# A fourth group of the down projection by seven products, with three chunks' token sums taken from DRAM

## The chip, the cores and the metric

The kernel runs on one core of a Trainium2 chip. Its engines work side by side, each through its own instruction list in order: TensorE multiplies (PE; its weight loads are shown as PEld), VectorE (DVE) and ScalarE (ACT) do elementwise work, GpSimd (POOL) and SyncE (SP) mostly issue transfers. The metric is the device time of one execution, in microseconds; lower is better. Three runs of the kernel before gave a median of 1541.31 us.

## The reference

One decoder layer for 256 tokens of width 2048: a mixer, then a gated MLP, then a final norm. The change touches the end of the MLP and the norm:

```python
h = rmsnorm(x, norm_ffn_w[l])
gate, up = jnp.split(jnp.einsum('bsd,df->bsf', h, w_up[l]), 2, axis=-1)
gate = causal_dwconv(gate, conv_ffn_w[l]) + conv_ffn_b[l]
x = x + jnp.einsum('bsf,fd->bsd', jax.nn.gelu(gate, approximate=False) * up, w_down[l])
return rmsnorm(x, norm_final_w)
```

The down projection `w_down` has 5632 rows and 2048 columns, in float32.

## The kernel before

**Float32 by two halves.** TensorE multiplies in a shorter format, so each weight block is split into a high part (`whi`, a cast on ScalarE, line 289) and a low part (`wlo`, the block less its high part, on VectorE, line 297). The activations are split too. A product of two float32 blocks is then three matmuls: high by high, high by low, low by high (`products`, line 1356). A weight block is 256 rows by 512 columns, 512 KB, and a matmul has 512 columns. `whi` and `wlo` have three buffers each: the cast for a block waits until TensorE has left the block three before it, and so TensorE is never more than two blocks behind the splits.

**The down projection.** The 5632 rows are eleven chunks of 512, and the 2048 columns two halves of 1024 (`half`, or `hf`). One chunk in one half is four blocks (two of rows, two of columns), and the tokens are two sets of 128. Most chunks are *plain*: each of the four blocks meets both token sets, 12 matmuls a block, 48 in all. The chunks in `SEVEN` take *seven products* instead of eight (Strassen's scheme in Winograd's form): three of the products use a block as it is (`11`, `22`, `21`), four use sums of blocks (`T1` to `T4`), and some use sums over the two token sets on the other side. A product is 6 matmuls, so such a chunk takes 42. For that VectorE makes four block sums in place (`quad`, line 283), and all seven operands are split, where a plain chunk has four splits. Once per chunk the token sums are made (`half_sums`, line 1292, with `four_sums`, line 1274): four sums, a cast, a low part; both halves use them. Before the change the chunk's activations are first put together again from their two parts (line 1299) for chunks 8 and 9, and chunk 10 keeps its float32 tile.

**The order of the work.** `stream` writes the order by hand: `gaps` is the number of plain blocks ahead of each group of seven products, and inside a group one plain block follows each product except the first. In the second half, four blocks of the last plain chunks are loaded and split early and kept (`keep`; `khi`, `klo`) for the end of the kernel. Within this order a scheduler at build time may let one engine's instruction go ahead of another's, as matmuls of neighbouring blocks do.

**Transfers.** Plain and kept blocks come by SP's queue into four buffers (`raw`, line 209). The blocks of the seven products (`quad`, line 243) are issued by POOL, whose list also holds the reload of the residual (`xt`, `xtl`, line 1555). There are eight homes for them; a group's block 11 and 12 take the homes of 22 and 21 of two groups back, and its 22 and 21 those of 12 and 11 of the group before. POOL waits at each issue until the home is free, and all that stands behind waits too.

**The end of a half.** When the last group of a half is through, a chain of four adds (`u`, lines 1575 to 1580) and four additions to the residual (`plus`, line 1504) joins the partial results. In the first half the finished columns are then multiplied by the final norm's weights (`weighted`, line 1511).

## Time and profile before

| | |
|---|---|
| median of three runs | 1541.31 us (1539.55 to 1541.64) |
| the profiled execution, whole | 1542.63 us |
| its span, first to last instruction | 1540.8 us |
| TensorE busy | 1526.0 us, 99% of the span |
| VectorE busy | 1253.4 us, 81% |
| ScalarE busy | 849.8 us, 55% |
| down projection, from its first matmul | 1299.0 us after the span's start |
| granted TensorE clock | 0.999 |

A row of the timeline gives the start and duration in microseconds, the engine, the line of the program, the operation, output and inputs, and in brackets the idle time before it with what ended it. A row of the chain of waits gives start, duration and the instruction that carried the end at that moment, with the number of instructions. A row of the windows gives the stretch, its length, and each engine's busy time in it with its instructions.

### The profile page before, as it was taken

How to read it: one execution, taken by the hardware profiler on the slowest of the kernel's cores; microseconds unless marked ns; L12 is line 12 of the kernel's file. 1: busy time of each engine (PE TensorE's matmuls, PEld its weight loads, DVE VectorE, ACT ScalarE, POOL GpSimd, SP SyncE). 2: the span in 40 equal slices, each digit the busy share in tenths (PEclk: the TensorE clock that was granted, in tenths of full speed). 3: DMA queues.
4: the chain of work that ended last, by engine and by line, in shares of the span. 5: the costliest groups of instructions: out<-in, count | busy, mean ns of one | idle time of the engine just before them, and what ended most of it. 6: DMA issues, size and time to landing. Idle time of an engine off the chain costs nothing.

```text
span 1540.8 us, 20209 instructions
## 1 busy us (share of the span) xinstructions
PE 1526.0 (99%) x7302; PEld 1257.4 (82%) x7302; DVE 1253.4 (81%) x1776; ACT 849.8 (55%) x1063; POOL 70.8 (5%) x90
## 2 busy tenths in 40 slices
PE   9999999999999999999999999999999999999998
PEld 8887888788878888788888888888788888888886
DVE  6788859896589858987667899999999886878885
ACT  7455446454455445454455676666667665555552
POOL 1010002000100000000000000000000000000100
PEclk9999999999999999999999999999999999999999
DMA  8776757776577766776578646666457467556652
GB/s 276 215 221 199 202 163 214 213 214 183 152 245 205 205 169 201 222 200 186 179 250 300 194 163 217 219 205 205 150 155 242 125 216 267 183 193 205 227 189 90
DMA packets 166674, 310.46 MB, mean 201 GB/s; under 512 B 19458, under 2 KB 23330, under 8 KB 166446
## 3 DMA queue, kind: packets, MB, share of 16 engines
q1 hardware_dynamic: 159456, 287.37, 60.0%
q0 software_dynamic: 5184, 18.88, 3.7%
q10 hardware_dynamic: 1934, 2.93, 0.5%
q8 instruction: 57, 0.93, 0.2%
q14 instruction: 43, 0.35, 0.1%
HBM read 301.75 MB, written 7.38 MB: 201 GB/s over the span
## 4 chain that ended last, share of the span: by engine, by line
PE 92%; DVE 4%; issue 2%; DMA 1%; ACT 0%; POOL 0%; POOLq 0%; DVEq 0%; ACTq 0%
PE psg L1374 25%; PE psm L334 15%; PE psm L332 14%; PE psm L333 14%; PE psm L1359 7%; PE psg L1359 7%; DVE wlo L297 3%; PE psm L1374 2%; PE psm L478 1%; PE psg L377 1%; DVE quad L230 1%; PE psm L1436 1%; DMA vrow<-ev 1%; PE psg L868 1%; DMA mv<-vrow 1%
## 5 line engine op out<-in xcount | busy, mean ns | idle before, releaser
L289 ACT CAST whi<-raw 128x1024 fp32r<-128x1024 f32 x428 | 450.0, 1052 | 428.4 <-PE psm L333 280.2
L297 DVE TENSOR_TENSOR wlo<-raw,whi 128x1024 fp32r<-128x1024 f32 x426 | 517.3, 1220 | 151.2 <-ACT whi L289 146.2
L289 ACT CAST whi<-quad 128x1024 fp32r<-128x1024 f32 x168 | 176.1, 1054 | 141.0 <-DVE quad L230 39.4
L297 DVE TENSOR_TENSOR wlo<-quad,whi 128x1024 fp32r<-128x1024 f32 x168 | 202.6, 1219 | 36.2 <-ACT whi L289 35.3
L334 PE MATMUL psm<-wlo,xhl 128*128 128x512 f32 x432 | 169.5, 393 | 1.6 <-DVE wlo L297 1.6
L332 PE MATMUL psm<-whi,xhl 128*128 128x512 f32 x432 | 169.0, 391 | 0.0
L333 PE MATMUL psm<-whi,xhl 128*128 128x512 f32 x432 | 168.6, 390 | 0.0
L1374 PE MATMUL psg<-whi,fhl 128*128 128x512 f32 x504 | 127.1, 389 | 0.0
L1374 PEld LDWEIGHTS psg<-whi,fhl 128*128 128x128 f32 x504 | 94.4, 188 | 19.5
L334 PEld LDWEIGHTS psm<-wlo,xhl 128*128 128x128 f32 x432 | 81.1, 188 | 19.0 <-DVE wlo L297 2.4
L333 PEld LDWEIGHTS psm<-whi,xhl 128*128 128x128 f32 x432 | 81.1, 188 | 16.8
L332 PEld LDWEIGHTS psm<-whi,xhl 128*128 128x128 f32 x432 | 81.1, 188 | 16.6
L230 DVE TENSOR_TENSOR quad<-quad,quad 128x1024 f32<-128x1024 f32 x72 | 87.6, 1217 | 0.0
L1374 PE MATMUL psg<-wlo,fhl 128*128 128x512 f32 x252 | 69.9, 389 | 0.0
L1374 PE MATMUL psg<-whi,ups 128*128 128x512 f32 x216 | 58.9, 394 | 0.0
L1359 PE MATMUL psm<-whi,hhi 128*128 128x512 f32 (+1 forms) x150 | 58.1, 387 | 0.0
L1359 PE MATMUL psm<-whi,hlo 128*128 128x512 f32 (+1 forms) x150 | 57.9, 386 | 0.0
L1359 PE MATMUL psm<-wlo,hhi 128*128 128x512 f32 (+1 forms) x150 | 57.4, 387 | 0.1
L1374 PEld LDWEIGHTS psg<-wlo,fhl 128*128 128x128 f32 x252 | 47.3, 188 | 9.8
L332 PE MATMUL psm<-whi,mhi 128*128 128x512 f32 x128 | 50.8, 397 | 0.0
L1359 PE MATMUL psg<-whi,hhi 128*128 128x512 f32 (+1 forms) x130 | 50.3, 387 | 0.4 <-ACT whi L289 0.4
L1359 PE MATMUL psg<-whi,hlo 128*128 128x512 f32 (+1 forms) x130 | 50.0, 386 | 0.0
(432 smaller groups left out, 2927.3 us busy)
## 6 DMA issues: line engine op xcount, KB each, us to landing
raw<-in_w_in_dram SPq DMA_DIRECT2D x224, 512.0 KB, 4.2
raw<-in_w_up_dram SPq DMA_DIRECT2D x104, 512.0 KB, 4.8
quad<-in_w_up_dram SPq DMA_DIRECT2D x72, 512.0 KB, 4.9
raw<-in_w_down_dram SPq DMA_DIRECT2D x64, 512.0 KB, 4.7
raw<-in_w_out_dram SPq DMA_DIRECT2D x32, 512.0 KB, 4.2
quad<-in_w_down_dram POOLq DMA_DIRECT2D x24, 512.0 KB, 5.5
mv<-vrow SPq DMA_DIRECT2D x12, 512.0 KB, 4.9
taps<-in_conv_qkv_w_dram SPq DMA_DIRECT2D x16, 256.0 KB, 6.8
```

The source lines that it names most:

```text
L230: nc.vector.tensor_tensor(out_, plus_, minus_, op=ALU.subtract)
L289: nc.scalar.copy(hi, raw)
L297: last_split[0] = nc.vector.tensor_tensor(lo, raw, hi.bitcast(F32), op=ALU.subtract).ins
L332: mm(ps[:, t, :], lh(k, t), hi[:, kk, :], start=(k == 0), stop=False)
L333: mm(ps[:, t, :], ll(k, t), hi[:, kk, :], start=False, stop=False)
L334: mm(ps[:, t, :], lh(k, t), lo[:, kk, :], start=False, stop=(k == nk - 1))
L377: nc.tensor.transpose(pt[:, ff, t * P : (t + 1) * P], src[:, t, f * P : (f + 1) * P], ident)
L478: mm(ps_k0[:, t, :], part(k, t), w[:, kk, :], start=(k == 0 and w is hi and part is xh), stop=(k == KD - 1 and w is lo))
L868: mm(pg0, kq[:, h, 0, 0:P], kq[:, h, :, :], start=True, stop=True)
L1359: mm(ps[:, cs], lhs(kk), part_[:, kk, cs], start=(first and kk == 0 and n == 0), stop=(last and kk == 1 and n == 2), skip_group_check=shared)
L1374: mm(ps, lhs(kk), w[n][:, kk], start=(first and n == 0 and kk == 0 and lhs is high), stop=False, skip_group_check=True)
L1436: nc.tensor.transpose(out_[f // 2][:, f % 2, t * P : (t + 1) * P], e[:, t, f * P : (f + 1) * P], ident)
```

## The change

A fourth chunk, number 7, leaves the plain ones and goes by seven products, in both halves. The first half takes the chunks in the order 8, 9, 10, 7, the second 7, 8, 9, 10. The number of plain blocks inside a group is no longer six: `FIVE` and `FOUR` say after which products one stands, so that groups have five, four or three, and the gaps between groups are shorter. The kept blocks move to after plain block 8, 12, 16 and 20 of the second half. The four activations that a seven-product chunk needs in float32 are no longer joined from two parts: chunks 7, 8 and 9 are written to DRAM when they are made and read back (`bring`) ahead of their token sums. The tile `x0`, which held the final norm's weights, now holds chunk 7's token sums; the weights are read later, on POOL's queue instead of ACT's, and the first half's columns are multiplied by them after the last split of the kernel.

```diff
-    SEVEN = (8, 9, 10)
+    SEVEN = ((8, 9, 10, 7), (7, 8, 9, 10))
...
-        for n, chunk in zip(gaps, SEVEN):
+        for (n, behind), chunk in zip(gaps, SEVEN[half]):
             plain(n)
             for i, what in enumerate(PRODUCTS):
                 steps[half].append(("part", chunk, what))
                 srcs.append((half, chunk, what))
-                if i:
+                if i in behind:
                     plain(1)
         plain(len(todo))
...
-    stream(0, DIRECT, (6, 3, 3))
-    stream(1, DIRECT[:-2], (3, 1, 1), (9, 13, 17, 21))
+    FIVE, FOUR = (1, 2, 3, 4, 5), (1, 3, 4, 6)
+    stream(0, DIRECT, ((6, FIVE), (1, FIVE), (1, FOUR), (1, (1, 3, 4))))
+    stream(1, DIRECT[:-2], ((3, FIVE), (0, FOUR), (0, FOUR), (0, FOUR)), (8, 12, 16, 20))
...
+    y_d = {c: dpool.tile([P, 4, S], F32, tag=f"y{c}", bufs=1, name=f"y{c}") for c in (7, 8, 9)}
+
+    def bring(c):
+        if c != 10:
+            whole[c] = fp.tile([P, 4, S], F32, tag={8: "hlo10", 9: "eu", 7: "y"}[c], name=nm("whole"))
+            nc.gpsimd.dma_start(whole[c], y_d[c])
...
-            h = fp.tile([P, 4, S], F32, tag="hlo10" if c == SEVEN[0] else "eu", name=nm("whole"))
-            nc.vector.tensor_tensor(h, hhi[c].bitcast(F32), hlo[c].bitcast(F32), op=ALU.add)
+            h = whole[c]
...
             nc.vector.tensor_tensor(y[:, fs], pt, y[:, fs], op=ALU.mult)
+        if c in y_d:
+            nc.gpsimd.dma_start(y_d[c], y)
...
-    nfin = big.tile([P, D], F32, tag="x0", name="nfin")
-    nc.scalar.dma_start(nfin, norm_final_w.partition_broadcast(P))
...
+            if hf and what == "22" and chunk == SEVEN[hf][1]:
+                nfin.append(big.tile([P, D], F32, tag="x0", name="nfin"))
+                nc.gpsimd.dma_start(nfin[0], norm_final_w.partition_broadcast(P))
+            if hf == 0 and what == "11" and chunk != SEVEN[0][-1]:
+                bring(SEVEN[0][SEVEN[0].index(chunk) + 1])
...
                     plus(t, c, own[c, t])
                     squared(t, c, c)
-                    weighted(t, c)
...
+    for t in range(2):
+        for c in range(2):
+            with tc.issue_after(last_split[0]):
+                weighted(t, c)
     ws += wk
```

Over the whole program TensorE's list loses 12 matmuls of 512 columns and VectorE's gains 17 instructions, ScalarE's gains seven casts and loses one transfer, SP's loses eight transfers of 512 KB and POOL's gains fifteen: eight `quad`, three writes and three reads of the chunks kept in DRAM, and the norm's weights. Nothing ahead of the down projection is moved except that these few stand in between.

Three places show it. The names are the program's, with the number of the buffer; `quad<-quad` with two tiles is a block sum, `wlo` the low part of a block, `klo` of a kept block, `raw` a plain block.

VectorE at the end of the first half's last group, from the split of product 21 on, before:

```order
L297 TENSOR_TENSOR wlo_11965<-quad_11752,whi_11963 128x1024
L1575 TENSOR_TENSOR u_12034<-u_12034,psg_11455 128x512
L297 TENSOR_TENSOR wlo_11977<-raw_11973,whi_11975 128x1024
L283 TENSOR_TENSOR quad_11752<-quad_11752,quad_11684 128x1024
L1576 TENSOR_TENSOR u_12034<-u_12034,psg_11426 128x512
L1504 SCALAR_TENSOR_TENSOR xt_11610<-u_12034,rs_7231,xt_11610 128x512
L1578 TENSOR_TENSOR u_12034<-u_12034,psg_11363 128x512
L297 TENSOR_TENSOR wlo_11994<-quad_11752,whi_11992 128x1024
L1580 TENSOR_TENSOR u_12034<-u_12034,psg_11363 128x512
L1504 SCALAR_TENSOR_TENSOR xt_11612<-u_12034,rs_7231,xt_11612 128x512
L297 TENSOR_TENSOR wlo_12008<-raw_12004,whi_12006 128x1024
```

And the same place after:

```order
L299 TENSOR_TENSOR wlo_12025<-quad_11866,whi_12023 128x1024
L1592 TENSOR_TENSOR u_12076<-u_12076,psg_11461 128x512
L285 TENSOR_TENSOR quad_11866<-quad_11866,quad_11817 128x1024
L1593 TENSOR_TENSOR u_12076<-u_12076,psg_11432 128x512
L1516 SCALAR_TENSOR_TENSOR xt_11560<-u_12076,rs_7231,xt_11560 128x512
L1595 TENSOR_TENSOR u_12076<-u_12076,psg_11369 128x512
L299 TENSOR_TENSOR wlo_12036<-quad_11866,whi_12034 128x1024
L1597 TENSOR_TENSOR u_12076<-u_12076,psg_11369 128x512
L1516 SCALAR_TENSOR_TENSOR xt_11562<-u_12076,rs_7231,xt_11562 128x512
L299 TENSOR_TENSOR wlo_12056<-raw_12052,whi_12054 128x1024
```

The split of a plain block between product 21 and the sum for T4 is gone: no plain block stands between these two products now.

VectorE at the end of the second half's second group and the start of the next, before:

```order
L297 TENSOR_TENSOR wlo_12497<-quad_12308,whi_12495 128x1024
L297 TENSOR_TENSOR wlo_12509<-raw_12505,whi_12507 128x1024
L283 TENSOR_TENSOR quad_12308<-quad_12308,quad_12249 128x1024
L297 TENSOR_TENSOR klo_12570<-raw_12566,khi_12568 128x1024
L297 TENSOR_TENSOR wlo_12526<-quad_12308,whi_12524 128x1024
L297 TENSOR_TENSOR wlo_12540<-raw_12536,whi_12538 128x1024
L297 TENSOR_TENSOR wlo_12558<-raw_12554,whi_12556 128x1024
```

And after:

```order
L299 TENSOR_TENSOR wlo_12459<-quad_12340,whi_12457 128x1024
L285 TENSOR_TENSOR quad_12340<-quad_12340,quad_12269 128x1024
L299 TENSOR_TENSOR wlo_12470<-quad_12340,whi_12468 128x1024
L299 TENSOR_TENSOR wlo_12490<-raw_12486,whi_12488 128x1024
L299 TENSOR_TENSOR wlo_12512<-quad_12363,whi_12510 128x1024
L285 TENSOR_TENSOR quad_12363<-quad_12398,quad_12363 128x1024
L285 TENSOR_TENSOR quad_12398<-quad_12431,quad_12398 128x1024
```

The sum for T4 and the low part of that sum now stand next to each other, and one plain block, not two, lies before the next group's product 11; the kept block's low part has moved to before T2's, ahead of these rows.

POOL in the second half, before:

```order
L243 DMA quad_12308<-in_w_down_dram 128x2x512
L243 DMA quad_12249<-in_w_down_dram 128x2x512
L1555 DMA xtl<-xtd 128x2x512 x2
L243 DMA quad_12373<-in_w_down_dram 128x2x512
L243 DMA quad_12432<-in_w_down_dram 128x2x512
```

And after:

```order
L245 DMA quad_12340<-in_w_down_dram 128x2x512
L245 DMA quad_12269<-in_w_down_dram 128x2x512
L1565 DMA nfin<-in_norm_final_w_dram 128x2048
L245 DMA quad_12363<-in_w_down_dram 128x2x512
L245 DMA quad_12398<-in_w_down_dram 128x2x512
L245 DMA quad_12472<-in_w_down_dram 128x2x512
L245 DMA quad_12431<-in_w_down_dram 128x2x512
L1572 DMA xtl<-xtd 128x2x512 x2
```

The norm's weights now stand between the blocks of the second group and those of the third, whose issues follow them on POOL.

More of the change, by code (lines that the diff above doesn't have):

```diff
@@ L149 @@
     down = [cols(w_down[0], 512 * c, KF) for c in range(4)]
-    SEVEN = (8, 9, 10)
+    SEVEN = ((8, 9, 10, 7), (7, 8, 9, 10))
     PRODUCTS = ("11", "T1", "22", "T3", "T2", "21", "T4")
-    DIRECT = [c for c in range(KF // 4) if c not in SEVEN]
+    DIRECT = [c for c in range(KF // 4) if c not in SEVEN[0]]
     LAST = DIRECT[-2:]
@@ L240, in next_quarter @@
             g, i = asked.pop(0)
-            half, chunk, what, home = g // 3, SEVEN[g % 3], ORDER[i], HOMES[g][i]
+            half, chunk, what, home = g // 4, SEVEN[g // 4][g % 4], ORDER[i], homes[g][i]
             r = (fp if home[:2] == "xt" else big).tile([P, 2, 512], F32, tag=home, name=nm("quad"))
@@ L1510, in weighted @@
     def weighted(t, c):
-        nc.vector.tensor_tensor(block(t, c), block(t, c), nfin[:, c * 512 : (c + 1) * 512], op=ALU.mult)
+        nc.vector.tensor_tensor(block(t, c), block(t, c), nfin[0][:, c * 512 : (c + 1) * 512], op=ALU.mult)
     def direct(ps, kp, t, w, first, last, **more):
@@ L1566 @@
             alone = what in ("11", "T1", "T2", "T3")
-            products(ps, high, low, w, alone and what not in began, alone and chunk == SEVEN[-1])
+            products(ps, high, low, w, alone and what not in began, alone and chunk == SEVEN[hf][-1])
             began.add(what)
-            if chunk == SEVEN[-1] and what == PRODUCTS[-1]:
+            if chunk == SEVEN[hf][-1] and what == PRODUCTS[-1]:
                 c0, c1 = 2 * hf, 2 * hf + 1
```

26 lines of the change are left out of this document (15 added, 11 removed).

## The prediction

> **What bounds the kernel now.** I read the page first: its span, the engines' busy times and the chain that ended last.
>
> ```profile
> span 1540.8 us, 20209 instructions
> PE 1526.0 (99%) x7302; PEld 1257.4 (82%) x7302; DVE 1253.4 (81%) x1776; ACT 849.8 (55%) x1063; POOL 70.8 (5%) x90
> ...
> PE 92%; DVE 4%; issue 2%; DMA 1%; ACT 0%; POOL 0%; POOLq 0%; DVEq 0%; ACTq 0%
> ```
>
> TensorE carries the end almost alone, so a matmul taken away is worth its whole spacing, provided that the splits keep up. Then I read the chain of waits over the down projection. Each row is a start, a length and the instructions that carried the end; the first is the projection's first block:
>
> ```profile
> 1299.01 2.73 PE psm L1359 x12
> ...
> 1332.09 19.04 PE psm L1359 x84
> ...
> 1366.09 19.04 PE psm L1359 x84
> ...
> 1408.75 0.49 DVE wlo L297
> ...
> 1442.90 1.23 DVE quad L283
> ...
> 1444.22 1.06 ACT whi L289
> ```
>
> 84 matmuls in 19.04 us are 0.2267 us each, twice the same. A product (6 matmuls) takes 1.36 us, a plain block (12) 2.72. Only twice does the chain leave TensorE here: at 1408.75 for a low part behind the first half's joining chain, at 1442.90 for a block sum and its cast. What the weight loads waited, from the waits of that engine over the down projection:
>
> ```profile
> PEld psg L1359 <- ACT whi L289: 0.8, 1, 0.8
> PEld psm L1359 <- DVE wlo L297: 0.6, 1, 0.6
> ```
>
> That is 1.4 us in all, some 1.2 of it lost (the loads behind a wait run closer together for a moment). The third view is VectorE's timeline at the first of these places, the end of the first half's third group:
>
> ```profile
> 1399.63 1.23 DVE L297 TENSOR_TENSOR wlo<-quad,whi 128x1024 fp32r<-128x1024 f32 x1 [1.04 <-ACT whi L289]
> 1400.77 0.68 DVE L1575 TENSOR_TENSOR u<-u,psg 128x512 f32<-128x512 f32 x1
> 1401.37 1.22 DVE L297 TENSOR_TENSOR wlo<-raw,whi 128x1024 fp32r<-128x1024 f32 x1
> 1402.50 1.22 DVE L283 TENSOR_TENSOR quad<-quad,quad 128x1024 f32<-128x1024 f32 x1
> 1403.64 0.68 DVE L1576 TENSOR_TENSOR u<-u,psg 128x512 f32<-128x512 f32 x1
> 1404.35 0.75 DVE L1504 SCALAR_TENSOR_TENSOR xt<-u,rs,xt 128x512 f32<-128x512 f32 x1
> 1405.02 0.68 DVE L1578 TENSOR_TENSOR u<-u,psg 128x512 f32<-128x512 f32 x1
> 1405.62 1.22 DVE L297 TENSOR_TENSOR wlo<-quad,whi 128x1024 fp32r<-128x1024 f32 x1
> 1406.76 0.68 DVE L1580 TENSOR_TENSOR u<-u,psg 128x512 f32<-128x512 f32 x1
> 1407.35 0.74 DVE L1504 SCALAR_TENSOR_TENSOR xt<-u,rs,xt 128x512 f32<-128x512 f32 x1
> 1408.02 2.35 DVE L297 TENSOR_TENSOR wlo<-raw,whi 128x1024 fp32r<-128x1024 f32 x2
> ```
>
> Behind one another, operations of 1024 columns start 1.14 us apart though each lasts 1.22 (1401.37, 1402.50, 1403.64), an add of 512 takes 0.60 and an addition to the residual 0.67. I count VectorE by these.
>
> **The change, part by part.** *TensorE.* A chunk goes from 48 matmuls to 42 in both halves: 12 x 0.2267 = 2.72 us less on the path. The Trainium skill, "TensorE: Matmul & The Clock Gate", section "Back-to-back issue gap", has some 131 ns a matmul of this width in a stream; by it the gain would be 1.6 us. The rows above measure 227, and the sum keeps 2.72.
>
> *VectorE.* Per half, four splits of plain blocks give way to seven splits of products and four block sums: over both halves 6 low parts and 8 sums more, 14 x 1.14 = 16.0 us. Chunk 7's token sums add four sums of 256 columns and a low part; two joins go. From the groups of lines over the down projection (busy time and mean of one in ns behind the bar):
>
> ```profile
> L283 DVE TENSOR_TENSOR quad<-quad,quad 128x1024 f32<-128x1024 f32 x24 | 29.3, 1221 | 0.4
> ...
> L1299 DVE TENSOR_TENSOR whole<-hhi,hlo 128x1024 f32<-128x1024 f32 x1 | 1.2, 1219 | 0.0
> ...
> L1281 DVE TENSOR_TENSOR sums<-whole 128x256 f32<-128x256 f32 x1 | 0.4, 418 | 0.0
> ```
>
> That is 4 x 0.34 + 1.14 - 2 x 1.14 = +0.2 us. So VectorE gets some 16 us more while TensorE gets 2.7 less, and this is what has to be hidden. ScalarE's seven more casts (1.06 each by the chain row) are 7 us on an engine at 55%.
>
> Where it lies, group by group (VectorE / TensorE): a second-half group of before, with six plain blocks, one in the gap and a kept one, 19 x 1.14 = 21.7 / 126 x 0.2267 = 28.6, 76%. A four-plain group with its kept block now, 16 x 1.14 = 18.2 / 20.4, 89%. The first half's last group with two blocks behind it, 18.2 + 5.1 (four adds, four additions) = 23.3 / 23.1, 101%. The second half's last, 23.3 / 20.4, with only the end's loads to catch up in. From the first half's third group to the last of all VectorE has 129 us of work in 139, 93%, though not evenly.
>
> What TensorE loses beside so full a VectorE, the up projection shows (windows: length, then PE, PEld, DVE busy), and the weight loads' waits over the same 300 us:
>
> ```profile
> 900.00:1000.00 100.00, 98.79 (x451) 81.35 (x450) 93.83 (x97) 67.10 (x79) 0.00 (x0) 1.00 0.55 183
> 1000.00:1100.00 100.00, 97.82 (x452) 80.01 (x451) 94.75 (x100) 67.62 (x78) 0.00 (x0) 1.00 0.51 172
> 1100.00:1200.00 100.00, 99.40 (x456) 82.21 (x455) 91.63 (x100) 66.75 (x78) 0.00 (x0) 1.00 0.63 202
> ```
>
> ```profile
> PEld psg L1374 <- DVE wlo L297: 7.1, 8, 1.1
> ```
>
> VectorE at 93.4% on average, 7.1 us of waiting: 2.4 per 100, so 3.3 us for 139. The same by places:
> - End of the first half. T4 now follows product 21 by 1.36 us instead of 4.08, while VectorE's way from 21's low part to T4's is shorter only by one split, 1.14. T4's low part, which came just in time before (ready at 1406.8; the next split was the 0.49 of the chain), comes 1.6 us closer. TensorE's list now puts four matmuls of high parts, 0.9, ahead of it: 0.7 lost, and some 0.4 more since the casts behind wait for T4's buffers. 1.1.
> - End of the second half: the same chain, with eight matmuls put ahead (1.8), but a split behind two of the joining operations: about 0.9.
> - The three boundaries with sum, cast and low part of T4 in a row: the rows at 1442.90 and 1444.22 give 2.4 us from the sum's start to the cast's end, so VectorE stands idle some 1.2; 18.2 + 1.2, and the wait for a kept block below, exceed 20.4 by up to 0.6. I take 0.4 each, 1.2.
> - Casts of kept blocks stand ahead of T2's cast on ScalarE and wait for their transfers:
>
> ```profile
> ACT khi L289 <- DMA raw<-in_w_down_dram: 4.7, 3, 2.7
> ```
>
> 1.6 us on average over the three; in a four-plain group T2's low part could be ready 10.0 us in, and is wanted at 12.2, so 2.2 to spare. 0.3.
>
> Together 3.5 us, against 3.3 by the up projection. The bounds are 0, as in two stretches of the first half of before, where TensorE was never idle,
>
> ```profile
> 1332.00:1366.00 34.00, 34.00 (x152) 28.15 (x151) 27.52 (x27) 17.62 (x18) 2.89 (x4) 1.00 0.60 203
> 1366.00:1400.00 34.00, 34.00 (x152) 28.15 (x151) 26.94 (x27) 17.99 (x19) 2.89 (x4) 1.00 0.60 199
> ```
>
> and 7.6 (the second rival). I take 3.5, which is built from this place's own rows.
>
> *Transfers.* The nearest rows to a write and a read of 512 KB on POOL are those of the residual (issue to landing), with the slowest of the `quad` loads behind; then the last product into chunk 8's tile, POOL's first `quad` issue, and VectorE's join of chunk 8, from which its sums began:
>
> ```profile
> xt<-xtd POOLq DMA_DIRECT2D x2, 512.0 KB, 6.0
> ```
>
> ```profile
> DMA to landing us min/median/max: 4.4/5.5/7.1
> ```
>
> ```profile
> 1241.14 1.28 DVE L1344 TENSOR_TENSOR y<-psm,y 128x512 f32<-128x512 f32 x2
> ```
>
> ```profile
> 1257.37 0.76 POOL L243 DMA_DIRECT2D quad<-in_w_down_dram  x1 [432.29 <-DVE wlo L297]
> ```
>
> ```profile
> 1277.62 1.22 DVE L1299 TENSOR_TENSOR whole<-hhi,hlo 128x1024 f32<-128x1024 f32 x1
> ```
>
> Chunk 8 is written and read back ahead of the `quad` issues: ready at 1242.4, two transfers and two issues (some 0.7 each) later it lies in its tile near 1256, 21 us before its sums, and POOL is free before 1257. Chunks 9 and 7 are asked for a group ahead of their use, some 20 us for 6. A block 22 is asked for when T3's low part frees its home, some 6 us into a group, and is wanted 20 us into it; with 0.7 of issue and the slowest landing of 7.1 there are 6 to spare. The norm's weights, 1 MB, stand ahead of the third group's blocks on POOL; they wait for product T2 of chunk 7, and the blocks behind them for T4 of the same group, which is later. I cost all of it at nothing; if that cover went, a late block 22 would hold VectorE's sums and so the whole group. Bytes per us stay: 9 blocks in 20.4 us instead of 12 in 28.6 (0.44 and 0.42). SP's queue has eight loads fewer.
>
> *The weighting.* Four multiplications leave the start of the second half and follow the last split:
>
> ```profile
> 1514.99 1.22 DVE L297 TENSOR_TENSOR wlo<-raw,whi 128x1024 fp32r<-128x1024 f32 x1 [0.59 <-ACT whi L289]
> 1518.66 0.75 DVE L1504 SCALAR_TENSOR_TENSOR xtl<-psg,rs,xtl 128x512 f32<-128x512 f32 x1 [2.45 <-PE psg L1359]
> ```
>
> VectorE waits 2.45 us there; 4 x 0.60 fits, and what follows waits for TensorE. Nothing.
>
> **The sum.** -2.72 for the matmuls, -1.2 for the two waits whose places are rewritten, +3.5: -0.4. The profiled execution took 1542.63 us, 1.3 above the median of the runs; it would take 1542.2, and the median goes from 1541.31 to 1540.9.
>
> **The rivals.**
> *No wait at all* (the order hides every split): -2.72 - 1.2 = -3.9, 1537.4. For it speaks the first half of before, without a wait at 81% of VectorE; against it 101% and 114% at the two ends.
> *VectorE becomes the bound*, and the kernel slower: its operations cannot overlap where sum, cast and low part alternate, so each costs its whole 1.22. A four-plain group is then 16 x 1.22 + 1.2 for T4's cast + 1.1 of the 1.6 for the kept block = 21.8, 1.4 over TensorE's 20.4; three of them 4.2. The first half's third group has 23.5 against 23.1, its last 25.1 against 23.1, 2.4 together, and the end's joining chain adds 1.0: 7.6. Net +3.7, 1545.0. It decides from the point where VectorE has no spare in a group, 20.4 us. For it speak 94.75% and 2.2 us lost in the worst window above; against it the starts 1.14 apart. The Trainium skill, "VectorE: DVE Perf Modes", section "The DRAIN you can't avoid", says that the next operation does not start until the pipe is empty, except where it is not held; by its first half the group would cost just these 1.22 each. The rows show the exception.
> *Kept blocks come later than now.* The landing times of plain and kept blocks on SP's queue between 1385 and 1500:
>
> ```profile
> DMA to landing us min/median/max: 3.6/5.3/6.9
> ```
>
> A kept block takes the buffer of the group's first plain block, free 2.9 us in, and its cast's turn comes at 6.5: with 5.3 it waits 1.7, with 6.9 it waits 3.3, over the 2.2 to spare by 1.1. Some 0.9 lost in each of three groups make 2.7: 1543.6. For it speaks the longest wait of 2.7 in the row above, against it that SP has eight loads fewer.
>
> That TensorE's work doesn't shrink is no rival: its list has 12 matmuls less.
>
> **How the numbers follow.** The forecast 0.60, no wait 0.14, VectorE as the bound 0.18, kept blocks 0.08. A difference of 0.2%, 3.1 us, is about what a measurement of this kernel can tell from none. Faster than 1538.2 is the no-wait case, 0.14; slower than 1544.4 are the VectorE case and a part of the last, 0.21; 0.65 remain. The range leaves out about half of the no-wait case and half of the VectorE case, 0.16: 1537.9 to 1545.2. Within the forecast alone, stalls of 2 to 5 us give 1539.4 to 1542.4.
>
> **What would show it.** TensorE's spacing still 0.227 us, 12 matmuls fewer; waits of its weight loads for low parts and casts in the down projection of about 3.5 us instead of 1.4, near 1410 and 1505 and at the ends of four-plain groups; VectorE near 93% busy from 1369 on; no wait for a `quad`, `whole` or `nfin` transfer. It would be wrong if these waits are under 1 us or over 6, if TensorE waits for POOL's transfers, or if the up projection moves.

## The result and the profile after

The changed kernel takes 1545.49 us (median of seven runs, 1544.26 to 1546.78), the kernel before 1540.73 us on the same chip. The ratio is 1.0031 with a 95% interval of 1.0019 to 1.0043: 4.8 us slower. That lies just above the predicted range (1537.9 to 1545.2), whose middle was no change.

The page of the changed kernel, its span, busy times and the shares of the chain that ended last; then three rows of that chain, the start, length and number of TensorE's matmuls in three undisturbed stretches:

```profile
span 1543.6 us, 20241 instructions
PE 1526.8 (99%) x7290; PEld 1254.0 (81%) x7290; DVE 1269.6 (82%) x1793; ACT 854.8 (55%) x1070; POOL 80.8 (5%) x105
...
PE 92%; DVE 4%; issue 1%; DMA 1%; ACT 1%; POOL 0%; POOLq 0%; ACTq 0%; DVEq 0%
```

```profile
1305.52 10.89 PE psm L1369 x48
...
1331.38 10.88 PE psm L1369 x48
...
1357.78 10.88 PE psm L1369 x48
```

48 matmuls in 10.88 us are 0.2267 us each, as before, and twelve are gone (7290 instead of 7302). So the loss is made of waiting. The waits of the weight loads from 1200 us on (total, times, longest):

```profile
PEld psm L1369 <- ACT whi L291: 4.6, 7, 1.6
PEld psg L1369 <- ACT whi L291: 3.5, 8, 0.9
PEld psg L1369 <- DVE wlo L299: 0.8, 1, 0.8
PEld psm L1369 <- DVE wlo L299: 0.2, 1, 0.2
```

Together 9.1 us, against 1.4 before. 8.1 of the 9.1 are waits for high parts, ScalarE's casts; before, it was 0.8 of the 1.4. What the waits cost is seen on the first and last matmul of the down projection, before and then after:

```profile
1298.85 0.39 PE L1359 MATMUL psm<-whi,hhi 128*128 128x512 f32 x1
1533.16 0.28 PE L1359 MATMUL psm<-klo,hhi 128*128 128x256 f32 x1
```

```profile
1298.13 0.39 PE L1369 MATMUL psm<-whi,hhi 128*128 128x512 f32 x1
1535.56 0.28 PE L1369 MATMUL psm<-klo,hhi 128*128 128x256 f32 x1
```

From 234.3 us it grew to 237.4, by 3.1. With the 2.72 of the matmuls, 5.8 us more are lost than before, and the waits grew by 7.7: a wait costs less than its length. The three rows of the chain show it at one place. From 1305.52 to 1331.38 TensorE makes 114 matmuls in 25.86 us without a wait; the next 114, with 0.84 us of waits among them, end at 1357.78 and take 26.40, only 0.54 more. The 3.1 us lie just inside the measured interval (2.9 to 6.6 us); what of the 4.8 goes beyond them, these two executions don't show.

Where the waits lie, from the timeline of the weight loads (start, and in brackets the wait before it):

```profile
1343.39 0.30 PEld L1369 LDWEIGHTS psg<-whi,sx 128*128 128x128 f32 x2 [0.20 <-ACT whi L291]
1344.33 0.19 PEld L1369 LDWEIGHTS psm<-whi,hhi 128*128 128x128 f32 x1 [0.64 <-ACT whi L291]
...
1370.73 0.19 PEld L1369 LDWEIGHTS psm<-whi,hhi 128*128 128x128 f32 x1 [0.64 <-ACT whi L291]
...
1386.41 0.19 PEld L1369 LDWEIGHTS psm<-whi,hhi 128*128 128x128 f32 x1 [0.65 <-ACT whi L291]
...
1411.50 0.19 PEld L1369 LDWEIGHTS psm<-whi,hhi 128*128 128x128 f32 x1 [1.60 <-ACT whi L291]
1414.07 0.19 PEld L1369 LDWEIGHTS psg<-whi,hhi 128*128 128x128 f32 x1 [0.88 <-ACT whi L291]
...
1493.44 0.19 PEld L1369 LDWEIGHTS psg<-whi,hhi 128*128 128x128 f32 x1 [0.53 <-ACT whi L291]
...
1512.51 0.19 PEld L1369 LDWEIGHTS psg<-wlo,hhi 128*128 128x128 f32 x1 [0.77 <-DVE wlo L299]
```

By places, all such rows added: product T1 of the first half's second and third groups 0.84 each (1343, 1370); the end of its third group 1.0 (1385, 1386) and the start of its fourth 0.4 (1394, 1396); the first half's end 3.0 (1410 to 1414); two boundaries of the second half 0.58 and 0.53; its end 1.9. Two thirds of the waiting is in the first half. VectorE's share from 1369 on, from the windows (length, then PE, PEld and DVE busy):

```profile
1369.00:1500.00 131.00, 128.64 (x558) 103.48 (x557) 117.32 (x109) 75.13 (x82) 14.99 (x21) 1.00 0.63 213
```

It is 90%, so on average VectorE is not full even where TensorE loses 2.4 us.

What ends late there is seen on VectorE and ScalarE at the first place, 1338 to 1345:

```profile
1338.56 1.22 DVE L1288 TENSOR_TENSOR sx<-sums,sx 128x1024 fp32r<-128x1024 f32 x1
1339.69 1.22 DVE L299 TENSOR_TENSOR wlo<-quad,whi 128x1024 fp32r<-128x1024 f32 x1
1340.95 2.48 DVE L285 TENSOR_TENSOR quad<-quad,quad 128x1024 f32<-128x1024 f32 x2
1343.37 1.23 DVE L299 TENSOR_TENSOR wlo<-quad,whi 128x1024 fp32r<-128x1024 f32 x1
```

```profile
1338.04 1.06 ACT L291 CAST whi<-quad 128x1024 fp32r<-128x1024 f32 x1
1342.28 1.05 ACT L291 CAST whi<-quad 128x1024 fp32r<-128x1024 f32 x1 [3.18 <-PE psm L1369]
1343.24 1.03 ACT L291 CAST whi<-raw 128x1024 fp32r<-128x1024 f32 x1
```

Read it as one chain. Product 11's block is cast at 1338.04, its low part runs at 1339.69, then the sum for T1, which is written over block 11 and so can't start before that low part, at 1340.95 (the row holds two sums, the first over at 1342.17), then T1's cast at 1342.28. TensorE loads T1's high part 0.06 us after that cast. From the start of 11's low part to the end of T1's cast are 3.6 us, and between these two products TensorE has one product, 1.36 us, to do. It begins with 11 at 1341.87, so it was 2.2 us behind 11's low part; this lead and the 1.36 cover 3.5 of the 3.6, and T1 is 0.20 late. ScalarE stood idle for 3.18 us ahead of this cast, and the plain block behind T1 queues behind it: its cast ends 0.94 us later, and TensorE waits a second time (0.64). The release that the row names is a buffer's; but the cast starts 0.11 us after the sum's end, as at 1408.50 below (0.10), where the row names the sum, and the experiments show that the sum counts. Product 21 and T4 are the same case, since T4's sum is written over block 21.

What eats the lead here stands in the first row: the low part of the next group's token sums lies on VectorE directly ahead of 11's low part, and in the same way at the second place (1370). In the 10.88 us up to that point VectorE has hardly a break:

```profile
1331.38:1342.26 10.88, 10.88 (x49) 9.01 (x49) 10.38 (x13) 4.77 (x5) 1.44 (x2) 1.00 0.61 205
```

It is 95% busy there, whatever the average says; one operation of 1.14 us less in front of the chain would have covered the 0.20. That is worked out from these rows: no run moves the token sums alone.

The first half's end in the same two views:

```profile
1405.43 1.23 DVE L299 TENSOR_TENSOR wlo<-quad,whi 128x1024 fp32r<-128x1024 f32 x1 [1.67 <-ACT whi L291]
1406.58 0.68 DVE L1592 TENSOR_TENSOR u<-u,psg 128x512 f32<-128x512 f32 x1
1407.18 1.22 DVE L285 TENSOR_TENSOR quad<-quad,quad 128x1024 f32<-128x1024 f32 x1
```

```profile
1408.50 1.05 ACT L291 CAST whi<-quad 128x1024 fp32r<-128x1024 f32 x1 [3.10 <-DVE quad L285]
1409.46 1.99 ACT L291 CAST whi<-raw 128x1024 fp32r<-128x1024 f32 x2
1412.97 1.05 ACT L291 CAST whi<-raw 128x1024 fp32r<-128x1024 f32 x1 [1.52 <-PE psm L1369]
```

21's low part, a joining add, T4's sum, T4's cast: 1405.43 to 1409.55, 4.1 us, with 1.36 us of TensorE work between the two products. Here VectorE stood idle for 1.67 us ahead of 21's low part, so it is the length of the chain and not VectorE's load.

### The profile page after: what moved, and what is told of

Same layout as the page of the kernel before. It is cut to its first block, busy times and chain, and to the rows that moved or that the text cites. A ratio compares the mean times of both kernels' runs of the same rounds, so it can differ in the third digit from the quotient of the medians.

```text
span 1543.6 us, 20241 instructions
## 1 busy us (share of the span) xinstructions
PE 1526.8 (99%) x7290; PEld 1254.0 (81%) x7290; DVE 1269.6 (82%) x1793; ACT 854.8 (55%) x1070; POOL 80.8 (5%) x105
## 4 chain that ended last, share of the span: by engine, by line
PE 92%; DVE 4%; issue 1%; DMA 1%; ACT 1%; POOL 0%; POOLq 0%; ACTq 0%; DVEq 0%
PE psg L1384 25%; PE psm L336 15%; PE psm L334 15%; PE psm L335 15%; PE psm L1369 7%; PE psg L1369 7%; DVE wlo L299 3%; PE psm L1384 2%; PE psm L480 1%; PE psg L379 1%; DVE quad L231 1%; PE psm L1446 1%; DMA mv<-vrow 1%; PE psg L870 1%; ACT whi L291 1%
## 5 line engine op out<-in xcount | busy, mean ns | idle before, releaser
L291 ACT CAST whi<-raw 128x1024 fp32r<-128x1024 f32 x420 | 441.3, 1052 | 419.9 <-PE psm L335 273.2
L299 DVE TENSOR_TENSOR wlo<-raw,whi 128x1024 fp32r<-128x1024 f32 x418 | 508.4, 1222 | 144.4 <-ACT whi L291 140.0
L291 ACT CAST whi<-quad 128x1024 fp32r<-128x1024 f32 x182 | 190.9, 1054 | 148.0 <-DVE quad L285 38.4
L299 DVE TENSOR_TENSOR wlo<-quad,whi 128x1024 fp32r<-128x1024 f32 x182 | 220.2, 1222 | 31.1 <-ACT whi L291 30.1
L1369 PE MATMUL psm<-whi,hhi 128*128 128x512 f32 (+1 forms) x140 | 54.9, 392 | 1.9 <-ACT whi L291 1.8
L1369 PE MATMUL psm<-whi,hlo 128*128 128x512 f32 (+1 forms) x140 | 54.1, 387 | 0.0
L1369 PE MATMUL psm<-wlo,hhi 128*128 128x512 f32 (+1 forms) x140 | 53.5, 387 | 0.0
L336 PE MATMUL psm<-wlo,mhi 128*128 128x512 f32 x128 | 50.0, 390 | 0.0
L335 PE MATMUL psm<-whi,mlo 128*128 128x512 f32 x128 | 49.9, 390 | 0.0
```

What stands on the lines that cost most here:

```text
L291: nc.scalar.copy(hi, raw)
L299: last_split[0] = nc.vector.tensor_tensor(lo, raw, hi.bitcast(F32), op=ALU.subtract).ins
L335: mm(ps[:, t, :], ll(k, t), hi[:, kk, :], start=False, stop=False)
L336: mm(ps[:, t, :], lh(k, t), lo[:, kk, :], start=False, stop=(k == nk - 1))
L1369: mm(ps[:, cs], lhs(kk), part_[:, kk, cs], start=(first and kk == 0 and n == 0), stop=(last and kk == 1 and n == 2), skip_group_check=shared)
```

## The experiments

Three theories stood at the start: A, VectorE has too much work in the denser groups; B, three buffers for high and low parts are too few to work ahead; D, TensorE's list asks for casts in another order than ScalarE makes them. Open was also which half and which part of the change costs what. Theory E, the chain, was formed after the first runs. Every ratio below is against the kernel before on the same chip, where it took 1541.1 to 1541.6 us.

**Each half alone.** `h0` has the fourth group in the first half only, `h1` in the second only (the order of the other half as before the change).

```diff
-    SEVEN = ((8, 9, 10, 7), (7, 8, 9, 10))
+    SEVEN = ((8, 9, 10, 7), (8, 9, 10))      # h0
+    SEVEN = ((8, 9, 10), (7, 8, 9, 10))      # h1
```

> The fourth group in the first half only; the second half has three groups with six plain blocks as before the change. Half of the matmuls go: 6 x 0.2267 = 1.36 us. If the loss lies in the first half's order (the waits counted there in the trace after: 0.84 + 0.84 + 1.2 + 3.2 = 6.1 us, 0.55 before), the time is 1540.7 - 1.4 + 5.5 = 1544.8 us and the weight loads wait about 6 us in the first half again. If instead the loss goes evenly with VectorE's added operations (7 of 14), it is half of 4.8: 1543.1 us. If the first half's waits come from the second half's demands (its blocks follow at once), they fall to under 3 us and the time is below 1542.

> The fourth group in the second half only. If the loss lies in the first half's order, this one is 1540.7 - 1.4 + (3.05 - 0.8) = 1541.6 us, with 0.5 us at each boundary of a four-plain group and about 1.9 us at the second half's end. If the loss goes evenly with VectorE's operations, 1543.1 us.

`h0`: 1545.76 us, 1.0033 (1.0020 to 1.0045), waits of 7.3 us. `h1`: 1543.66 us, 1.0020 (1.0010 to 1.0030), waits of 5.4 us. The first half's order alone costs as much as the whole change, though it saves only half of the matmuls; it was forecast at 1544.8. `h1` was forecast at 1541.6 and took 2.1 more. The halves don't add: in `h1` two group starts of the second half wait (1.0 and 1.4 us at 1425 and 1449) that don't wait in the kernel after. Which boundary waits depends on how the work arrives there.

**VectorE's work, or TensorE's order.** `nosum` leaves all 32 block sums of the down projection out; `peorder` holds TensorE to the program's order.

```diff
-                nc.vector.tensor_tensor(raw, plus, minus, op=ALU.subtract)     # nosum
```

```diff
-    pe_order.close()        # peorder: moved from ahead of the two halves to behind them
...
+    pe_order.close()
     ws = []
```

> The kernel after without the block sums on VectorE: T1 to T4 split a single block instead of a sum, so the output is another one; 32 operations of 1024 columns are gone, all casts, low parts, transfers and matmuls stay. If VectorE has too much work at the boundaries (theory A), the weight loads wait under 2 us in the down projection and the time is about 1545.5 - 7.5 = 1538 us. If the casts' order against TensorE's list makes the waits (theory D), the first half's end keeps its 3.2 us and the time is 1541 to 1542. If the few split buffers alone make them (theory B), about 5 us of waits remain, 1541 to 1543.

> The kernel after with TensorE kept to the order in which the program is written through the down projection, so that no matmul of a later block stands ahead of an earlier one. Theory D (TensorE's list asks for casts out of ScalarE's order): the 3.2 us at the first half's end fall to under 1.5 and those at the second half's end from 1.9 to about 1; the time is 1543 us. Theories A and B: the waits stay or grow, since the filler matmuls are gone too, 1545.5 us or above.

`nosum`: 1540.82 us, 0.9999 (0.9990 to 1.0009), waits of 2.9 us, all behind the casts of two kept blocks that waited 3.9 and 1.9 us for their loads. `peorder`: 1547.10 us, 1.0041 (1.0028 to 1.0054), waits of 11.2 us, 9.1 of them now for low parts. Theory D falls: without the interleaved list the waits are 2.1 us more, not fewer (the times' intervals overlap). The sums do make them, but this doesn't tell whether by their number or by their place.

**A fourth buffer, and the change's other parts alone.** `buf4` adds a fourth pair of buffers in the place of chunk 9's token sums, which are not made, so VectorE has five operations less, ahead of the second group. `bounce` and `lateweight` put one part each into the kernel before: the chunks in DRAM, and the late weighting. `nobounce` takes the DRAM chunks out of the kernel after.

```diff
+            if keep is None and len(made) >= DOWN0 + 8 and (len(made) - DOWN0) % 4 == 0:     # buf4
+                fourth = big.tile([P, 2, 2, 512], F32R, tag="x3", name=nm("w4"))
```

```diff
-            nc.vector.tensor_tensor(h, hhi[c].bitcast(F32), hlo[c].bitcast(F32), op=ALU.add)     # bounce
+            h = whole[c]
...
-                    weighted(t, c)                                                               # lateweight
...
-            nc.gpsimd.dma_start(whole[c], y_d[c])                                                # nobounce
+            nc.vector.tensor_tensor(whole[c], hhi[c].bitcast(F32), hlo[c].bitcast(F32), op=ALU.add)
```

> The kernel after with a fourth pair of buffers for the high and low parts in the down projection from its ninth block on, and splits that may run one block further ahead. Its place is that of chunk 9's token sums, for which chunk 8's are used, so the output is another one and five operations of VectorE are gone. Theory B (VectorE and ScalarE can't work ahead with three buffers): the waits of the weight loads fall from 9.1 to under 3 us, 1539 to 1540 us. Theory A (too much VectorE work at the boundaries): a block of lead absorbs the 0.5 to 0.8 us of the inner boundaries but not the ends: 1542 to 1543. Theory D: the ends keep their 3.2 and 1.9 us, 1542 to 1543.

> The kernel before with one part of the change: chunks 8 and 9 are kept in DRAM and read back ahead of their token sums instead of being joined from two parts on VectorE. By the prediction the transfers cost nothing and VectorE loses two operations: 1540.7 us, within 1 us, and no wait for a whole transfer. If POOL's list makes the blocks behind it late: 1542 or more.

> The kernel before with one part of the change: the first half's columns are multiplied by the norm's weights after the last split instead of at the start of the second half. By the prediction this costs nothing at the end; four operations of 0.6 us leave the start of the second half, where the kernel before waited 0.55 us for a low part: 1540.2 to 1540.7 us. If the end is longer by the four multiplications: up to 1543.

> The kernel after with chunks 8, 9 and 7 joined from their two parts on VectorE again, as before the change; 3 x 1.14 us of VectorE work come back in the first half, at the end of the gap before groups 1, 2 and 3 or inside them. Theory A: each moves the waits at the first half's boundaries by up to 1.1 us, 1546.5 to 1548 us. If DRAM's transfers themselves delay something, faster than 1545.5. Theories B and D: 1545.5 within 0.7.

`buf4`: 1542.45 us, 1.0006 (0.9997 to 1.0014). Of the first half's waits 0.5 us are left, 5.4 us remain in the second. At the second group the token sums that are not made may have a part in it; at the third group and at the end it is one block more of lead that hides the waits. So B is right that lead is short, but more lead doesn't end it. `bounce`: 1541.11, 0.9999 (0.9990 to 1.0007); `lateweight`: 1541.81, 1.0002 (0.9993 to 1.0011), though its profile shows 4.3 us of waits, all but 0.6 after the casts of three kept blocks, which waited 3.9, 2.2 and 3.5 us for their loads; `nobounce`: 1545.34, 1.0025 (1.0016 to 1.0034), like the kernel after. These parts cost nothing that can be measured. The Trainium skill, "Perfetto Trace Analysis", section "Optimization Strategy", says that the same gap repeated on the busy engine can mean too few buffers. A fourth buffer takes the waits from 9.1 to 5.9 us, so the trace agrees in part: what the lead has to cover is not told by the gap.

**Number or place.** `drop14` leaves out the sums of T1 and T4, `drop23` those of T2 and T3: 16 operations of VectorE each. T1 and T4 are the two whose sum is written over the block of the product just before them.

```diff
-                nc.vector.tensor_tensor(raw, plus, minus, op=ALU.subtract)
+                if srcs[len(made)][0] == "up" or srcs[len(made)][2] in ('T2', 'T3'):     # drop14; drop23: ('T1', 'T4')
+                    nc.vector.tensor_tensor(raw, plus, minus, op=ALU.subtract)
```

> The kernel after without the block sums of T1 and T4 (16 operations of VectorE); those of T2 and T3 stay. The two products split a single block, so the output is another one. Theory E: the chains are cut, waits under 3 us as without any sums, 1540 to 1541 us. Theory A: half of the effect of all sums, waits of about 6 us, 1543 us.

> The kernel after without the block sums of T2 and T3 (16 operations of VectorE as well); those of T1 and T4 stay. The output is another one. Theory E: the chains are whole, waits stay at 8 us or more, 1545 to 1546 us. Theory A: the same as without the sums of T1 and T4, 1543 us.

`drop14`: 1541.44 us, 1.0004 (0.9995 to 1.0012). `drop23`: 1545.34 us, 1.0029 (1.0018 to 1.0040). The waits of `drop23`, and then the kept blocks' casts in `drop14`:

```profile
PEld psg L1370 <- ACT whi L292: 6.0, 12, 0.9
PEld psm L1370 <- ACT whi L292: 4.0, 6, 1.5
PEld psg L1370 <- DVE wlo L300: 1.5, 2, 0.8
PEld psm L1370 <- DVE wlo L300: 0.2, 1, 0.2
```

```profile
ACT khi L292 <- DMA raw<-in_w_down_dram: 9.6, 4, 3.4
```

Theory A falls as a matter of the total: the same number of operations is taken away, and only those in the chain matter. 16 operations of 1.14 us outside of it leave the time where it was. By places, `drop23` has the same 0.84 us at both group starts, and of the first half's 6.1 us 5.5 are left; in the second half 2.5 us are new, behind a kept block's cast that waited 2.8 for its load. (The Trainium skill, "VectorE: DVE Perf Modes", section "Rules for kernel authors", advises for chained VectorE operations to make fewer of them; here 16 fewer don't help where they stand outside the chain.) `drop14` nearly met its expected time (1540 to 1541) but not its expected waits, 6.0 us instead of under 3: with the chains cut, casts of kept blocks wait 9.6 us for their loads, and TensorE waits behind some of them.

**The chains drawn apart.** `apart` keeps all the work and changes only the numbers of the order: a plain block (2.72 us of TensorE work) now stands between 11 and T1 and between 21 and T4. `apart0` does so in the first half alone.

```diff
-    stream(0, DIRECT, ((6, FIVE), (1, FIVE), (1, FOUR), (1, (1, 3, 4))))
-    stream(1, DIRECT[:-2], ((3, FIVE), (0, FOUR), (0, FOUR), (0, FOUR)), (8, 12, 16, 20))
+    stream(0, DIRECT, ((5, (0, 2, 3, 4, 5)), (1, (0, 2, 3, 4, 5)), (1, (0, 2, 3, 5)), (1, (0, 2, 3, 5))))
+    stream(1, DIRECT[:-2], ((3, (0, 2, 3, 4, 5)), (0, (0, 2, 3, 5)), (0, (0, 2, 3, 5)), (0, (0, 2, 3, 5))), (8, 12, 16, 20))
```

> The kernel after with the same work in another order: a plain block now stands between product 11 and T1 and another between 21 and T4, in every group of both halves, instead of after T1 and T3 or T4; the gaps ahead of the first half's groups are 5, 1, 1, 1 instead of 6, 1, 1, 1 and each group there has one plain block more or as many. Theory E (T1's sum is written over block 11 and T4's over block 21, so low part of 11, sum, cast, in a chain of 1.14 + 1.22 + 1.06 = 3.4 us, stands against one product of 1.36 us): the weight loads wait under 2 us in the down projection, and the time is 1541 - 2.7 - 1.2 + 1 = 1538 us. Theory A (too much VectorE work) and theory B (too few buffers): no operation and no buffer is different, waits of 6 us or more remain, 1543 to 1546 us.

> The same new order in the first half alone. Theory E: the 6.1 us of waits of the first half fall to under 1, the second half keeps its 3 us or gets up to 1 more at its start: 1540 to 1541 us. Theories A and B: 1544 to 1546 us.

`apart`: 1541.71 us, 1.0001 (0.9992 to 1.0010), waits of 3.8 us. `apart0`: 1542.54 us, 1.0006 (0.9997 to 1.0015): one wait of 0.5 us is left in the first half, where 6.1 had been, and 5.6 us in the second half, some 2.5 more than in the kernel after, so it missed its 1540 to 1541. Theory E holds for the chains, but `apart` missed its 1538 by 3.7 us. Most of what was left, 2.7 of 3.8 us, stands behind a kept block's cast, which waits for its own load (ScalarE), and TensorE behind it:

```profile
1452.91 1.05 ACT L291 CAST khi<-raw 128x1024 fp32r<-128x1024 f32 x1 [3.81 <-DMA raw<-in_w_down_dram]
```

```profile
1454.95 0.19 PEld L1369 LDWEIGHTS psg<-whi,hhi 128*128 128x128 f32 x1 [1.85 <-ACT whi L291]
```

**The same cause without the change.** `gap0` is the kernel before, with no operation added, and three plain blocks fewer ahead of its second and third group (one instead of four between T4 and the next product 11):

```diff
-    stream(0, DIRECT, (6, 3, 3))
+    stream(0, DIRECT, (12, 0, 0))
```

> The kernel before, with the same work and three groups, and only the first half's gaps changed from 6, 3, 3 to 12, 0, 0: one plain block instead of four stands between T4 of a group and the next group's product 11. Theory E: product T1 of the second and third group waits behind its chain as in the kernel after, 0.84 to 1.5 us each, 1.7 to 3 us together: 1543 to 1544.5 us, with no fourth group and no operation added. If the added operations are what costs: 1541 us, no new wait.

`gap0`: 1543.84 us, 1.0012 (1.0003 to 1.0021), with the two new waits where they were expected:

```profile
1359.35 0.30 PEld L1359 LDWEIGHTS psg<-whi,sx 128*128 128x128 f32 x2 [0.83 <-ACT whi L289]
1360.29 0.19 PEld L1359 LDWEIGHTS psm<-whi,hhi 128*128 128x128 f32 x1 [0.65 <-ACT whi L289]
1385.75 0.30 PEld L1359 LDWEIGHTS psg<-whi,sh 128*128 128x128 f32 x2 [0.19 <-ACT whi L289]
1386.70 0.19 PEld L1359 LDWEIGHTS psm<-whi,hhi 128*128 128x128 f32 x1 [0.65 <-ACT whi L289]
```

It is the lead ahead of a chain that decides, not the added work: the chain and the token sums in front of it are those of the kernel before, and the plain blocks that hid them are gone.

**What the kept blocks wait for.** `nfinlate` is the kernel after with the 1 MB read of the norm's weights moved behind the last blocks; `apart2` is `apart` with the same; `apart3` has the kept blocks one plain block earlier as well; `apart4` and `apart5` have them after plain blocks 6, 10, 14 and 18, with and without the moved read.

```diff
-            if hf and what == "22" and chunk == SEVEN[hf][1]:      # nfinlate, apart2, apart3, apart4
+            if hf and what == "22" and chunk == SEVEN[hf][3]:
...
-    (8, 12, 16, 20))
+    (7, 11, 15, 19))      # apart3
+    (6, 10, 14, 18))      # apart4, apart5
```

> The kernel after with only the read of the norm's weights moved to the end of the second half. In its trace the kept blocks wait 2.0 us once and TensorE does not wait behind them, so by the chain theory (E) nothing changes: 1545.5 us within 0.7. If the read slows the second half's loads at a cost: 1543 to 1544.

> The spread-out order in both halves, and the read of the norm's weights moved from the second group of the second half to its end, ahead of the last block. If that read of 1 MB delays a kept block's load (the trace shows raw loads of 8.8 us, median, beside it, 5.9 elsewhere in that stretch), the 2.7 us of waits at 1455 go, about 1.1 us of waits remain in the down projection, and the time is 1541.7 - 2.4 = 1539 us, faster than both kernels. If the kept block's place is the cause, 1541.7 us with the same waits.

> As the one with the read moved, and the kept blocks one plain block earlier (7, 11, 15, 19). If the read was the cause: the same 1539 us within 0.7. If the kept block's place was: faster than it by up to 2 us.

> The spread-out order with the late read, and the kept blocks after plain blocks 6, 10, 14 and 18 of the second half, so that the four raw buffers come free well before a kept block's load is asked for. If the kept block's load was the cause, no cast of a kept block waits for a transfer, the waits of the weight loads in the down projection are under 1 us, and the time is 1541 - 2.7 - 1.2 + 0.6 = 1537.7 us, 1537 to 1539, faster than both kernels. If another resource holds the time, 1540.5 us or above as in the two runs before it.

> The same with the read of the norm's weights where the change had put it. If that read costs nothing (as moving it in the kernel after showed), the same time within 0.7 us; if it collides with the kept blocks' loads, slower by 1 us or more and a kept block's cast waits near 1450.

`nfinlate`: 1544.95 us, 1.0023 (1.0013 to 1.0032), the same waits as the kernel after to 0.1 us. `apart2`: 1540.71, 0.9999 (0.9991 to 1.0008); the wait of 1.8 us stays. So the read is not the cause. `apart3`: 1544.16, 1.0020 (1.0011 to 1.0029); the wait moves to the third kept block, 3.1 us, which neither theory had said. `apart4`: 1538.23, 0.9977 (0.9968 to 0.9986); `apart5`: 1537.91, 0.9980 (0.9971 to 0.9989). Both beat both kernels, by the forecast made from the waits. All waits of the weight loads in the down projection of `apart5`:

```profile
PEld psm L1369 <- ACT whi L291: 0.5, 1, 0.5
PEld psm L1369 <- DVE wlo L299: 0.3, 1, 0.3
```

and ScalarE's waits for a block sum in the kernel after, and in `apart5`:

```profile
ACT whi L291 <- DVE quad L285: 38.4, 14, 3.4
```

```profile
ACT whi L291 <- DVE quad L285: 18.1, 9, 2.9
```

Why the place matters can be read from the built order and the times of the loads. A kept block needs no `whi` buffer, and the scheduler puts its cast ahead of plain blocks that are loaded before it. SP's loads in `apart` around the second kept block (`raw_12485`), and ScalarE's casts of the same blocks:

```
L210 DMA raw_12399<-in_w_down_dram 128x2x512
L210 DMA raw_12426<-in_w_down_dram 128x2x512
L210 DMA raw_12473<-in_w_down_dram 128x2x512
L210 DMA raw_12485<-in_w_down_dram 128x2x512
```

```
L291 CAST khi_12487<-raw_12485 128x1024
L291 CAST whi_12401<-raw_12399 128x1024
...
L291 CAST whi_12428<-raw_12426 128x1024
...
L291 CAST whi_12475<-raw_12473 128x1024
```

The fourth to be loaded is the first to be cast. There are four `raw` buffers, so its load takes the buffer of the block loaded four before it, and VectorE's low part of that block and SP's issue in `apart` are these two rows:

```profile
1446.91 1.22 DVE L299 TENSOR_TENSOR wlo<-raw,whi 128x1024 fp32r<-128x1024 f32 x1
1448.16 0.37 SPq L210 DMA_DIRECT2D raw<-in_w_down_dram  x1
```

The load is issued 0.03 us after that low part ends. ScalarE's turn for the cast comes at 1449.10, 0.94 us after the issue, and the cast starts 4.75 after it. In `apart5` the same kept block stands ahead of one plain block; its load is issued at 1437.22 and its cast starts at 1445.86, 8.6 us later and without a wait. In `apart4` and `apart5` each kept block stands ahead of one, and the longest wait is 0.4 us. In `drop14` and `nosum` the longest waits (3.4 and 3.9) are again at kept blocks ahead of three. With two ahead the wait goes from 0 to 2.7 us in the kernels before and after, but to 3.9 in `lateweight` and once to 4.8 in `apart3`, so the count is not the whole of it: that load of `apart3` was issued at 1461.79, 4.0 us ahead of its cast's turn, and its cast started 8.8 after the issue. Beside it POOL had the residual's reload and two `quad` loads under way, which took 9.3 us (median) to land. Whether these slowed it no run tells, and none moves the kept blocks in the kernel after with its order left as it is.

## Why the prediction was wrong

The median was to go to 1540.9 us and went to 1545.5. By its steps:

- **Twelve matmuls, -2.72 us: right.** The spacing is 0.2267 us before and after.
- **Two waits that vanish, -1.2: right.** The 9.1 us are all that wait now, so the 1.4 of before has to be taken off, as was done; both places wait again, but among the new ones.
- **New waits, 3.5 us: this step failed.** They are 9.1 us, and what they cost in the two traces, 3.1 (the stage's growth) + 2.72 (the matmuls) + 1.2 (the waits of before) = 7.0, is twice the 3.5. "Over 6" had been named as a sign of being wrong. Of the places named, the two inner boundaries of the second half were near (0.4 each, measured 0.58 and 0.53). The end of the first half was 1.1 and measured 3.0, the end of the second 0.9 and measured 1.9, the third T4 boundary 0.4 and measured 1.0.
- **The first half's group starts, costed at nothing: wrong by 1.7 us of waits.** The prediction took the stretches of before in which TensorE never idled as the lower bound. There, four plain blocks stood between T4 and the next product 11. `gap0` takes three of them away without adding any work and gets waits at the same two places (1.48 and 0.84 us, against 0.84 and 0.84).
- **How the 3.5 was made.** A busy share (93.4%) and the up projection's loss beside it were used as a cross-check, and both agreed, by chance. From 1369 to 1500 VectorE was 117.3 of 131 us busy, 90%, so that was near; but `drop23` has 16 operations less and loses just as much. The average share was not what set the waits; ahead of the two group starts it is 95%. The chain of sum and cast had been seen (2.4 us, at 1442.90 and 1444.22 of before) but was priced as idle time of VectorE at three places, not as a latency of 3.6 to 4.1 us against 1.36 us of TensorE's work, and the lead, at each T1 and T4. At the first half's end T4's own cast makes 0.5 of the 3.0 us; the rest is the plain blocks' casts that queue behind it.
- **VectorE as the bound (the rival at 1545.0) had the time, not the mechanism.** Most of its operations still start 1.14 us apart (1338.56, 1339.69). A sum behind the low part that it has to wait for does start 1.26 after it (1339.69, 1340.95), as this rival had it, but that is 0.1 a time. The total of its work doesn't set the time (`drop14` against `drop23`); what stands just ahead of a chain counts.
- **Kept blocks later (the rival at 1543.6): not in the changed kernel,** where TensorE waits behind none of them, but it was the next limit once the chains were gone: 3.2 us between `apart` and `apart5` by their ratios (1.0001 and 0.9980).
- **Transfers and weighting at nothing: right.** No engine waited for a `quad`, `whole` or `nfin` transfer in the kernel after, and `bounce`, `nobounce`, `nfinlate` and `lateweight` differ from their neighbours by less than they can tell.

## What to carry to other kernels

Where one block's operand is made in place over the previous block's, count the latency from that block's split to the next block's cast through every engine, and set it against the work that the matrix engine has between the two, plus the lead that the buffers allow. An average busy share hides what stands just ahead of that chain. The waits added up are more than what they cost; the first and last instruction of the stage tell the cost. A wait-free stretch is no lower bound for another order of the same work, since its lead may be what the change spends. Before giving up on an algorithm that saves work, move the independent blocks into the chain: the same instructions in another order turned a loss of 4.8 us into a gain of some 3.

## What was not expected of the hardware

- **One late operand costs two waits.** Product T1's high part makes TensorE wait 0.20 us and the next block's 0.64 more, because ScalarE's two casts of 1.05 us, one behind the other, end 0.94 apart, while the loads between take only 0.30. The Trainium skill, "ScalarE: Activation LUTs", section "What ACT_TABLE_LOAD costs", says that ACTIVATEs behind one another overlap by some 93 ns; the operations here, casts in the trace's words, start 0.96 us apart (1342.28, 1343.24) and last 1.05, which agrees.
- **Handing over is cheap, the length of the chain is not.** From the end of a sum to the start of its cast 0.10 to 0.11 us, from the end of a cast to the weight load 0.05 to 0.06. Nearly all of the 3.6 us is the operations themselves.
- **Executions of one kernel scatter by 2.5 to 5 us** (`apart4`: 1536.15 to 1539.47 in eleven runs, `gap0`: 1540.68 to 1545.63 in eleven), about as much as the changes studied here. In the single profiles much of that lies ahead of the stage: the down projection starts between 1296.2 (`apart0`) and 1299.8 us (`nfinlate`). Its own length, from first matmul to last, is steadier: 237.4 and 237.5 us in the kernel after and `nfinlate`, 233.7 and 233.7 in `apart` and `apart2`, 231.1 and 231.1 in `apart4` and `apart5`, each pair differing in the read of the norm's weights alone.
